# Layer 0 of a two-layer decoder step: the conv-gate and conv-input products of each width tile as seven block products instead of two full ones

## The chip, the core and the metric

The kernel runs on one core of a Trainium2 chip. Its engines have queues of their own: TensorE (PE, matmuls; PEld is its weight load), VectorE (DVE), ScalarE (ACT), GpSimd (POOL) and SyncE (SP, which issues most transfers). The metric is the device time of one execution in microseconds (us), the median of several runs.

## What is computed

One inference step of a trunk of two layers: 512 prompt positions and 8 sample sequences of 8 positions, 576 columns in all, through layer 0 (a gated short convolution) and layer 1 (an mLSTM block). The change is in the input half of layer 0:

```
hnorm = rmsnorm(x, norm_w[0])                             # x: 576 positions x 1024
b_gate, c_gate, xa, z = jnp.split(hnorm @ w_in, 4, -1)    # w_in: 1024 x 8192, 2048 each
u = c_gate * xa
conv, new_buf = causal_dwconv(u, buf, conv_w)             # 3 taps along the positions
y = b_gate * conv * jax.nn.silu(z)
x = x + y @ w_out                                         # w_out: 2048 x 1024
```

All data are fp32.

## The kernel before

Activations lie with 128 features on the partitions and the 576 positions along the free side; 1024 features are 8 such tiles, the width of 2048 is 16 (`NW`). Weights come in chunks of 512 KB (`io["wts"][c]`): 1024 input features by 128 output features. Layer 0 has chunks 0 to 63: width tile f uses chunk 4f for `c_gate`, 4f+1 for `xa`, 4f+2 for `z` and 4f+3 for `b_gate`. Chunks 64 to 79 are its output projection, from 80 on layer 1.

fp32 products are made of three reduced ones (fp32r): each operand is split into a rounded high part and the rest, and hi*hi, hi*lo and lo*hi are added. ScalarE makes the high part of half a chunk (L195, `wh<-wr`, 128x512), VectorE the rest (L196, `wl<-wr,wh`); four such pairs of buffers rotate. A chunk's product (`gemm`, `products`, `step`) is 8 feature tiles by 3 parts by two matmuls of 256 and 320 columns (L210): 48 matmuls into one accumulator `acc` of two PSUM banks. Two accumulators rotate, and loads run ahead in four raw buffers `wr`.

The norm's scale per position is not applied to the input, but as `rb` to products (`rb2`, its square, to `c_gate*xa`). Chunks 0 to 3 are multiplied while the norm is still being summed, and copied to `raws`. Then the loop over f issues, in this order: chunk 4f+4 (`c_rows(f + 1)`, scaled from PSUM to `cr`, L486), chunk 4f+1 (`u = acc * cr`, L504), the convolution of u (L405 to L411), chunk 4f+2 (`z`, L510, silu L511), chunk 4f+3 (`cv = acc * cv`, L513, then times z, L514), and `split(cv)` (L152, L153), which keeps the rows for the output projection.

Layer 1 already uses block products for its v, k and q projections. `gemm_pair` takes two chunks as a 2x2 block matrix (two chunks by even and odd feature tiles) and the activations as another (even and odd feature tiles by first and last 288 positions), for half of the input features; the other half goes the plain way (L340). `forms` prepares sums and differences of the activation blocks, `block_weights` loads the two chunks and makes two sums `ws` (L267, L268), `parts_of` splits a block of weights (L238, L239), and `block_pair` issues the seven products, each 4 tiles by 3 parts by one matmul of 288 columns (L284), and combines the four result blocks with VectorE additions and ScalarE copies of 288 columns.

The order on each engine is set when the program is built: instructions are recorded in the order of the code and placed by a scheduler that has its own idea of their lengths, and each engine then works its queue strictly in that order. PSUM has eight banks: four one-bank buffers in a pool that lasts the whole program (`psum`, tag `b1`), and four banks in a pool that `accumulators` closes and opens again for a stage.

## Time and profile before

| what | before |
|---|---|
| median of 3 runs (range) | 1739.17 us (1736.37 to 1743.02) |
| profiled execution: time / span | 1740.33 us / 1738.2 us |
| granted TensorE clock, mean | 0.987 |
| PE busy / DVE busy / ACT busy | 1694.7 us (97%) / 1005.3 us (58%) / 647.7 us (37%) |
| DMA moved | 275.23 MB, mean 158 GB/s |

The profiled execution is one run, of which every instruction was recorded; it is 1.2 us above the median. A matmul's record is longer than its share of the engine, since matmuls overlap; the price of one is read from starts that follow each other. Layer 0's input half covers about the first 420 us, its output projection the next 100 us (its last rows are stored at 523 us).

### The profile page before, as it was taken

The numbers are of one execution on the slowest core, as the hardware profiler recorded it, in microseconds if no ns is written. First come the engines' busy times: TensorE is split into PE (matmuls) and PEld (weight loads), VectorE is DVE, ScalarE is ACT, GpSimd is POOL, SyncE is SP. The second block draws the span as 40 slices with busy tenths as digits, with TensorE's granted clock in tenths as the row PEclk, the third lists the DMA queues.
The fourth block names the chain that finished last, engine by engine and source line by source line (L and its number), as shares of the span: only waits on it lengthen the run. The fifth ranks groups of instructions, "written<-read, shape, count | busy, mean of one in ns | idle before, by whom it ended". The sixth has DMA issues, their size and how long they took to land. (4 is left out here: it accounts for less than half of the span.)

```text
span 1738.2 us, 30944 instructions
## 1 busy us (share of the span) xinstructions
PE 1694.7 (97%) x12483; PEld 1615.4 (93%) x12483; DVE 1005.3 (58%) x1864; ACT 647.7 (37%) x1172; POOL 104.7 (6%) x241
## 2 busy tenths in 40 slices
PE   9999999999999999999999999999999998998998
PEld 9999999999999999999899989899898787888898
DVE  5644445444335997555755436355367566677755
ACT  5222222222323554333434224233245455555421
POOL 0000000000001000000111010100011000000000
PEclk9999999999999999999999999999999899999999
DMA  5232222222432435344432463452745588797973
GB/s 190 86 93 76 87 89 86 92 76 95 140 126 93 129 107 176 107 150 122 152 116 95 150 203 118 168 175 85 240 159 203 170 289 288 251 327 268 366 287 104
DMA packets 107487, 275.23 MB, mean 158 GB/s; under 512 B 11057, under 2 KB 33457, under 8 KB 107345
## 3 DMA queue, kind: packets, MB, share of 16 engines
q1 hardware_dynamic: 91984, 255.95, 44.7%
q10 hardware_dynamic: 15360, 17.32, 2.9%
q8 instruction: 98, 1.61, 0.4%
q14 instruction: 45, 0.36, 0.1%
HBM read 211.13 MB, written 62.09 MB: 157 GB/s over the span
## 5 line engine op out<-in xcount | busy, mean ns | idle before, releaser
L210 PE MATMUL acc<-hi,wh 128*128 128x256 f32 (+1 forms) x1968 | 427.8, 299 | 10.0 <-ACT z L804 6.8
L210 PE MATMUL acc<-hi,wl 128*128 128x256 f32 (+1 forms) x1968 | 426.3, 298 | 0.0
L210 PE MATMUL acc<-lo,wh 128*128 128x256 f32 (+1 forms) x1968 | 425.7, 298 | 0.0
L195 ACT CAST wh<-wr 128x512 fp32r<-128x512 f32 x342 | 211.1, 620 | 514.4 <-PE acc L210 396.9
L210 PEld LDWEIGHTS acc<-hi,wh 128*128 128x128 f32 x1968 | 333.5, 191 | 14.5 <-ACT z L804 7.0
L196 DVE TENSOR_TENSOR wl<-wr,wh 128x512 fp32r<-128x512 f32 x342 | 234.1, 688 | 188.2 <-ACT wh L195 183.2
L210 PEld LDWEIGHTS acc<-hi,wl 128*128 128x128 f32 x1968 | 332.8, 191 | 2.8 <-issue 1.7
L210 PEld LDWEIGHTS acc<-lo,wh 128*128 128x128 f32 x1968 | 333.2, 191 | 0.7 <-issue 0.5
L284 PE MATMUL p<-hi,wh 128*128 128x288 f32 x576 | 171.1, 301 | 0.9 <-DVE xm L557 0.9
L340 PE MATMUL p<-hi,wh 128*128 128x288 f32 x736 | 170.2, 299 | 0.0
L284 PE MATMUL p<-lo,wh 128*128 128x288 f32 x576 | 169.2, 295 | 0.0
L284 PE MATMUL p<-hi,wl 128*128 128x288 f32 x576 | 166.1, 295 | 1.2 <-DVE wl L239 1.2
L340 PE MATMUL p<-lo,wh 128*128 128x288 f32 x736 | 167.3, 295 | 0.0
L340 PE MATMUL p<-hi,wl 128*128 128x288 f32 x736 | 166.7, 297 | 0.2 <-DVE wl L196 0.2
L340 PEld LDWEIGHTS p<-hi,wh 128*128 128x128 f32 x736 | 121.1, 188 | 14.7 <-issue 11.2
L340 PEld LDWEIGHTS p<-hi,wl 128*128 128x128 f32 x736 | 121.1, 188 | 4.6 <-issue 2.9
L238 ACT CAST wh<-wr 128x512 fp32r<-128x512 f32 x96 | 59.6, 620 | 175.1 <-PE p L340 117.4
L340 PEld LDWEIGHTS p<-lo,wh 128*128 128x128 f32 x736 | 121.8, 188 | 0.0
L284 PEld LDWEIGHTS p<-hi,wh 128*128 128x128 f32 x576 | 108.0, 188 | 5.0 <-ACT k L329 2.5
L284 PEld LDWEIGHTS p<-lo,wh 128*128 128x128 f32 x576 | 108.5, 188 | 0.0
L284 PEld LDWEIGHTS p<-hi,wl 128*128 128x128 f32 x576 | 107.1, 188 | 1.4 <-DVE wl L239 1.4
L1052 DVE SCALAR_TENSOR_TENSOR c<-c,cols,r 128x512 f32<-128x512 f32 x128 | 91.1, 743 | 27.2 <-PE r L1051 21.0
(363 smaller groups left out, 2276.3 us busy)
## 6 DMA issues: line engine op xcount, KB each, us to landing
wr<-wts SPq DMA_DIRECT2D x222, 512.0 KB, 3.6
c<-cs SPq DMA_DIRECT2D x112, 512.0 KB, 5.8
cs_out<-c SPq DMA_DIRECT2D x64, 512.0 KB, 6.6
x<-xT SPq DMA_DIRECT2D x16, 288.0 KB, 4.2
xcs<-xc ACTq DMA_DIRECT2D x16, 288.0 KB, 2.1
x<-xcs SPq DMA_DIRECT2D x16, 288.0 KB, 4.1
x<-x1s SPq DMA_DIRECT2D x16, 288.0 KB, 4.8
ld<-xcs SPq DMA_DIRECT2D x16, 288.0 KB, 8.4
```

The source lines that it names most:

```text
L195: last_act[0] = nc.scalar.copy(hi, raw[:, 4 * i:4 * i + 4, :]).ins
L196: nc.vector.tensor_tensor(lo, raw[:, 4 * i:4 * i + 4, :], hi.bitcast(F32), ALU.subtract)
L210: nc.tensor.matmul(acc[:, o:o + j - i], a[:, k % 4, :], x[:, i:j], start=(first and k == 0 and p == 0), stop=(last and k == 7 and p == 2))
L238: last_act[0] = nc.scalar.copy(hi, src).ins
L284: nc.tensor.matmul(bank_, a[:, j, :], x, start=(start and j == 0 and i == 0), stop=(j == 3 and i == 2), skip_group_check=True)
L340: nc.tensor.matmul(b, a[:, k % 4, :], x[:, t:t + HT], start=bool(new) and k == 0 and i == 0, stop=(k == 7 and i == 2), skip_group_check=True)
L1052: ins = nc.vector.scalar_tensor_tensor(ct[:, j, :], ct[:, j, :], dec[:, o + j:o + j + 1], r, ALU.mult, ALU.add).ins
```

## The change

Width tile 0 stays as it was. Chunks 4 and 5 are made as before, but copied to scratch tiles `cx`. For the width tiles 2 to 15, chunks 4f and 4f+1 are made by one `block_pair` over all 1024 input features (`xs=None`: no plain part), one f ahead, and its four result blocks fill the two tiles `cx`. Since both factors now lie in SBUF, `gated` scales and multiplies them there; it and the steps of the convolution are put in a list `work`, from which `block_pair` takes one after each of five of its products. Chunks 4f+2 and 4f+3 stay plain products of 48 matmuls.

The activation blocks that the seven products need are made at the start of the layer (`first_blocks`, four times, from x times the norm's weight). The program-wide PSUM pool is gone: the one-bank buffers belong to each stage's pool, and layer 0 has three pools in turn, `acc0` up to chunk 5, `acc0a` (two accumulators and four one-bank blocks) for the loop, and `acc0b` from the output projection on. Scratch tiles of layer 0 (`X`, seven buffers) lie in the pool of the load buffers, which is closed and opened again at the output projection.

```diff
-        psum = ctx.enter_context(tc.tile_pool(name="psum", bufs=4, space=PSUM))
+        layer0 = [False]
+        def X(n=NT, name="x"):
+            if not layer0[0]:
+                return T(n, name=name)
+            uid[0] += 1
+            return loads[1].tile([P, n], F32, name=f"{name}{uid[0]}", tag="X", bufs=7)
...
-            return psum.tile([P, 512], F32, name=f"{name}{uid[0]}", tag="b1", bufs=4)
+            return accs[1].tile([P, 512], F32, name=f"{name}{uid[0]}", tag="b1", bufs=4)
...
+        def mixed(xa, xb):
             a, b = T(name="fa"), T(name="fb")
             nc.vector.tensor_tensor(a[:, 0:HT], xa[:, 0:HT], xa[:, HT:NT], ALU.subtract)
             nc.vector.tensor_tensor(a[:, HT:NT], xb[:, HT:NT], a[:, 0:HT], ALU.add)
             nc.vector.tensor_tensor(b[:, 0:HT], xa[:, HT:NT], xb[:, HT:NT], ALU.subtract)
             nc.vector.tensor_tensor(b[:, HT:NT], xb[:, 0:HT], a[:, HT:NT], ALU.subtract)
+            return split(a), split(b)
...
-        def block_pair(c1, c2, fs, xs, out1, out2, add, mid=None, then=None):
+        def block_pair(c1, c2, fs, xs, out1, out2, add, mid=None, then=None, pops=0):
...
             product(b0, parts_of(a11), "b11", True)
             nc.scalar.copy(p, b0)
+            run(pops)
...
+            elif xs is None:
+                nc.scalar.copy(o11, b0)
+                tt(o21, b3, u, ALU.add)
...
+        def first_blocks(j):
+            for x, i in ((xs[2 * j], 2 * j), (xs[2 * j + 1], 2 * j + 1)):
+                nc.vector.tensor_scalar(x, x, col("norm0", i), None, ALU.mult)
+            b11 = [x[:, 0:HT] for x in h1[2 * j]]
+            fs.append(blocks_of(*mixed(xs[2 * j], xs[2 * j + 1]), b11, h1[2 * j + 1]))
...
         raw_product(mm("acc"), w2)
         rc = [rms_columns([ssq[:, 288 * i:288 * i + 288]], 96) for i in range(2)]
+        first_blocks(0)
         raw_product(mm("acc"), w3)
...
+        first_blocks(1)
...
         for f in range(NW):
...
+            work.append(gated)
+            work.extend(conv_steps(cv, u, ext_f, [col("ca0", f), col("ca1", f), col("ca2", f)]))
+            work.append(saved)
+            zb = [raw_weights(4 * f + i) for i in (2, 3)] if f else None
+            if f + 1 < NW:
+                cx = [X(name="cx") for _ in range(2)]
+            if f == 0:
+                for i in range(2):
+                    acc = mm("acc")
+                    products(acc, weights(4 + i), h1, True, True)
+                    nc.scalar.copy(cx[i], flat(acc))
+                    if i:
+                        block_weights(8, 9)
+                    first_blocks(2 + i)
+                accumulators("acc0a", bufs=2)
+            elif f + 1 < NW:
+                block_pair(4 * f + 4, 4 * f + 5, fs, None, *cx, False, pops=1)
+            run(len(work))
+            if 0 < f < NW - 2:
+                block_weights(4 * f + 8, 4 * f + 9)
...
-            cr = next_cr
-            if f + 1 < NW:
-                next_cr = c_rows(f + 1)
-            xa = product(1)
...
+        accumulators("acc0b", bufs=2)
+        load_buffers("loads1", 4)
+        layer0[0] = False
```

The built program shows what stands where. On PE the rows go from 11857 to 11689. The first place is VectorE's queue in the middle of the loop, from the row that reads the `b_gate` product out of PSUM. In a row, `wl<-wr,wh` is the low half of a plain or block weight, `lo` that of the finished rows. Before:

```order
L513 TENSOR_TENSOR cv_1973<-acc_2044,cv_1973 128x576
L196 TENSOR_TENSOR wl_2178<-wr_2171,wh_2177 128x512
L514 TENSOR_TENSOR cv_1973<-cv_1973,z_2040 128x576
L153 TENSOR_TENSOR lo_2106<-cv_1973,hi_2105 128x576
L196 TENSOR_TENSOR wl_2243<-wr_2240,wh_2242 128x512
L486 TENSOR_TENSOR cr_2109<-acc_2110,rb_470 128x576
L196 TENSOR_TENSOR wl_2247<-wr_2240,wh_2246 128x512
L196 TENSOR_TENSOR wl_2306<-wr_2303,wh_2305 128x512
L504 TENSOR_TENSOR u_2229<-acc_2170,cr_1851 128x576
L196 TENSOR_TENSOR wl_2310<-wr_2303,wh_2309 128x512
L406 COPY ext_1333<-u_2229 128x8x8
L409 SCALAR_TENSOR_TENSOR cv_2231<-u_2229,cols,cv_2231 128x511
```

And now at the same place (`ws` are the weight sums, `pu` and `p` the scratch and a PSUM block of `block_pair`):

```order
L581 TENSOR_TENSOR cv_2075<-acc_2287,cv_2075 128x576
L251 TENSOR_TENSOR wl_2417<-wr_2219,wh_2416 128x512
L582 TENSOR_TENSOR cv_2075<-cv_2075,z_2284 128x576
L251 TENSOR_TENSOR wl_2438<-wr_2220,wh_2437 128x512
L160 TENSOR_TENSOR lo_2347<-cv_2075,hi_2346 128x576
L542 TENSOR_TENSOR u_2350<-cx_2081,cx_2080 128x576
L251 TENSOR_TENSOR wl_2457<-wr_2220,wh_2456 128x512
L319 TENSOR_TENSOR cx_2356<-pu_2358,p_2359 128x288
L437 COPY ext_1520<-u_2350 128x8x8
L326 TENSOR_TENSOR cx_2357<-pu_2358,p_2396 128x288
L251 TENSOR_TENSOR wl_2477<-ws_2224,wh_2476 128x512
L440 SCALAR_TENSOR_TENSOR cv_2351<-u_2350,cols,cv_2351 128x511
```

The four plain splits of this stretch are now four splits of block weights, the scaled `cr` has gone, and two result blocks `cx` have come between u and the convolution.

The second place is VectorE's queue at the start of the layer, from the row of the squared scale `rb2`. Before, a plain split and the first gated rows followed it:

```order
L479 TENSOR_TENSOR rb_470<-rb_451 128x576
L196 TENSOR_TENSOR wl_627<-wr_620,wh_626 128x512
L486 TENSOR_TENSOR cr_473<-raw_307,rb_470 128x576
L486 TENSOR_TENSOR cr_477<-acc_478,rb_470 128x576
L504 TENSOR_TENSOR u_538<-raw_309,cr_473 128x576
```

Now two rows follow it, `rb_499<-rb_464` at L527 itself and the first of the mixed activation blocks (`fa_570<-x_127`, L257), and then these, up to the second weight sum `ws` of the first pair of chunks:

```order
L259 TENSOR_TENSOR fb_571<-x_127,x_129 128x288
L541 TENSOR_TENSOR raw_304<-raw_304,rb_499 128x576
L541 TENSOR_TENSOR cx_506<-cx_506,rb_499 128x576
L258 TENSOR_TENSOR fa_570<-x_129,fa_570 128x288
L260 TENSOR_TENSOR fb_571<-x_129,fa_570 128x288
L160 TENSOR_TENSOR lo_577<-fa_570,hi_576 128x576
L160 TENSOR_TENSOR lo_581<-fb_571,hi_580 128x576
L257 TENSOR_TENSOR fa_654<-x_131 128x288
L259 TENSOR_TENSOR fb_655<-x_131,x_133 128x288
L286 TENSOR_TENSOR ws_648<-wr_645 128x512
L258 TENSOR_TENSOR fa_654<-x_133,fa_654 128x288
L287 TENSOR_TENSOR ws_649<-ws_648,wr_644 128x512
```

The two last pairs of mixed blocks `fa` and `fb`, their low halves `lo` and the two sums `ws` have moved in front of the first weights of the first block product.

More of the change, by code (lines that the diff above doesn't have):

```diff
@@ L197, in split_weights, with raw_weights, weights @@
             return hi, lo
-        def weights(chunk, keep=False):
+        def raw_weights(chunk):
             raw = weight_tile()
             latest[0] = load(out=raw, in_=io["wts"][chunk]).ins
+            return raw
+        def weights(chunk, keep=False, raw=None):
+            if raw is None:
+                raw = raw_weights(chunk)
             return [split_weights(raw, i, keep) for i in range(2)]
@@ L298, in block_pair @@
                 tt(o12, p, b1, ALU.subtract)
+            run(pops)
             product(b0, parts_of(a12), "b21", False)
@@ L399, in rms_spread, with conv_steps, first, tap @@
             return acc
-        def conv(cv, u, ext, taps):
+        def conv_steps(cv, u, ext, taps):
             n = len(taps)
             h = n - 1
-            nc.scalar.activation(cv, u, AF.Copy, scale=taps[h])
-            nc.vector.tensor_copy(ext[:, :, h:h + 8], u[:, NP:NT].rearrange("p (b t) -> p b t", t=8))
             cs = cv[:, NP:NT].rearrange("p (b t) -> p b t", t=8)
-            for s in range(1, n):
+            def first():
+                nc.scalar.activation(cv, u, AF.Copy, scale=taps[h])
+                nc.vector.tensor_copy(ext[:, :, h:h + 8], u[:, NP:NT].rearrange("p (b t) -> p b t", t=8))
+            def tap(s):
                 nc.vector.scalar_tensor_tensor(cv[:, s:NP], u[:, 0:NP - s], taps[h - s], cv[:, s:NP],
@@ L411, in conv @@
                 nc.vector.scalar_tensor_tensor(cs, ext[:, :, h - s:h - s + 8], taps[h - s], cs, ALU.mult, ALU.add)
+            return [first] + [lambda s=s: tap(s) for s in range(1, n)]
+        def conv(*args):
+            for go in conv_steps(*args):
+                go()
         load(out=cols, in_=io["cols"])
```

48 lines of the change are left out of this document (28 added, 20 removed).

## The prediction

> **What bounds the kernel now.** I read the page first, then the busy times by stretch, then the stage of the change in time order. Columns of the stretches: length, busy us (and instructions) of PE, PEld, DVE, ACT, POOL, granted clock, DMA share, GB/s.
>
> ```profile
> PE 1694.7 (97%) x12483; PEld 1615.4 (93%) x12483; DVE 1005.3 (58%) x1864; ACT 647.7 (37%) x1172; POOL 104.7 (6%) x241
> 100.00:200.00 100.00, 100.00 (x752) 100.00 (x752) 48.32 (x80) 28.35 (x44) 2.32 (x4) 1.00 0.28 87
> 200.00:300.00 100.00, 100.00 (x752) 100.00 (x752) 47.17 (x79) 27.09 (x42) 2.32 (x4) 1.00 0.28 84
> 640.00:660.00 20.00, 18.65 (x135) 17.79 (x134) 20.00 (x47) 10.64 (x18) 0.00 (x0) 1.00 0.33 113
> 820.00:840.00 20.00, 20.00 (x155) 20.00 (x154) 14.82 (x30) 8.95 (x17) 0.00 (x0) 1.00 0.49 165
> 860.00:880.00 20.00, 20.00 (x154) 20.00 (x153) 17.61 (x35) 8.85 (x16) 4.03 (x8) 1.00 0.43 126
> ```
>
> In the stage of the change (100 to 300 us) PE never stops at full clock, VectorE is busy under half the time, DMA a quarter. So a matmul taken away is time taken away, as long as its replacement keeps PE fed. The last three rows lie in layer 1, where the same block products run: PE stays full with VectorE 74% and 88% busy, and loses 1.35 of 20 us only with VectorE busy all the time. That is the scale for what follows.
>
> **PE's share of the change.** A pair of plain products is 2 x 48 matmuls of 288 columns on average; seven block products are 7 x 12 = 84 of 288. Fourteen width tiles change: 14 x 12 = 168 matmuls go, the difference of PE's rows in the built program (11857 to 11689). A plain one costs 100 / 752 = 0.133 us. A block one, from the starts in layer 1:
>
> ```profile
> 657.40 0.29 PE L284 MATMUL p<-lo,wh 128*128 128x288 f32 x1
> ...
> 658.47 0.29 PE L284 MATMUL p<-hl,wl 128*128 128x288 f32 x1
> ```
>
> Eight steps in 1.07 us, 0.134 each: the same. The gain is 168 x 0.133 = **22.3 us**, 1.6 per pair, if PE stays full.
>
> **VectorE in the loop.** Records overlap, so I price it from starts that follow each other without idle:
>
> ```profile
> 631.13 0.75 DVE L153 TENSOR_TENSOR lo<-xm,hi 128x576 fp32r<-128x576 f32 x1
> 631.80 0.75 DVE L409 SCALAR_TENSOR_TENSOR xc<-xm,cols,xc 128x511 f32<-128x511 f32 x1
> 632.46 0.28 DVE L411 SCALAR_TENSOR_TENSOR xc<-ext,cols,xc 128x64 f32<-128x64 f32 x1
> 632.65 0.69 DVE L239 TENSOR_TENSOR wl<-wr,wh 128x512 fp32r<-128x512 f32 x1
> ...
> 637.50 0.69 DVE L196 TENSOR_TENSOR wl<-wr,wh 128x512 fp32r<-128x512 f32 x1
> 638.10 0.69 DVE L268 TENSOR_TENSOR ws<-ws,wr 128x512 f32<-128x512 f32 x1
> ...
> 641.02 0.46 DVE L310 TENSOR_TENSOR pu<-p,pu 128x288 f32<-128x288 f32 x1
> 641.39 0.45 DVE L314 TENSOR_TENSOR v<-p,v 128x288 f32<-128x288 f32 x1
> ```
>
> So 0.67 us for 576 columns, 0.60 for 512, 0.37 for 288, 0.66 and 0.20 for the convolution's two kinds. Per width tile before: 8 weight splits, 7 rows of 576, 4 convolution rows and a copy (0.1): 4.8 + 4.7 + 1.8 = 11.3 us of 192 x 0.133 = 25.5. After: 11 splits (7 block, 4 plain) and 4 weight sums, 15 x 0.60 = 9.0; six block additions 2.2; seven rows of 576 4.7; convolution 1.8: 17.7 us of 180 x 0.133 = 23.9, 74%. ScalarE gets 3 more casts and two copies of 288: at most 3 x 0.62 + 2 x 0.40 = 2.7 us per tile on an engine busy 28%, no bound. DMA moves the same bytes.
>
> A share of 74% still needs slack at each place. Put t = 0 where PE begins a pair. It runs p6, p1, p5 (1.6 each, split during the plain products), the first two matmuls of p4 (to 5.1), the second halves of p1 (to 6.6), p4 (8.0), p6 (9.6), p5 (11.2), then z (17.6) and b_gate (23.9). VectorE at t = 0 stands at the read of the b_gate accumulator (L581, the first row shown in the order): it can't pass it before PE is done, and four block splits are queued behind it. Adding up from 0.2: L581 to 0.9, split of a12 to 1.5, L582 2.1, a21 2.7, the finished rows 3.4 (behind a cast), u 4.1, a22 4.7, two result blocks and a copy, s2 6.1. PE wants them at 5.1, 8.0, 6.6 (a22's low half) and 9.6: the tightest, a22, has 1.9 us, about 1.4 if the cast makes VectorE wait. The two plain splits (7.6 and 9.6) are wanted at 11.2 and 14.4. So nothing waits; I take 0.5 us for the whole loop, between 0 and the upper end of the second rival.
>
> The loads: a raw buffer is free when a22 is split (t = 4.7); SP then issues the next pair's second chunk, which L286 (the first weight sum) reads at 8.4.
>
> ```profile
> DMA to landing us min/median/max: 3.3/3.5/4.4
> ```
>
> It lands at 8.0 to 9.1 (the weight loads from 40 to 400 us). VectorE may wait 0.7 there, with a plain split behind it that has 4.8 us of slack: hidden. If a landing took over 8 us, PE would wait. SP's order otherwise only shifts; the loads of chunks 65 to 67 stand behind `cpa_out`, which waits for POOL's copy from u(15), made 12 us before. POOL's work is the same.
>
> **The seam at the start.** Sixteen block rows, eight scalings and eight splits of the mixed blocks (16 x 0.37 + 16 x 0.67 = 16.6 us, a scaling priced like the other rows of 576) are new on VectorE ahead of the first pair, where it was busy 15.5 of 28 us:
>
> ```profile
> 21.00:49.00 28.00, 28.00 (x218) 28.00 (x218) 15.53 (x31) 11.14 (x21) 1.86 (x3) 1.00 0.26 83
> 41.88 0.39 PE L210 MATMUL acc<-lo,wh 128*128 128x320 f32 x1
> 42.57 0.76 DVE L479 TENSOR_TENSOR rb<-rb 128x576 f32<-128x576 f32 x1 [2.71 <-ACT rb L477]
> ```
>
> PE's order up to chunk 5 is unchanged; after the second norm spread (41.88) 51 matmuls remain, so PE is free at 48.7. VectorE starts `rb2` at 42.57, and 14 rows stand from it to the second weight sum: five of 576, seven of 288, two of 512 = 7.1 us, ready at 49.8 with its pipeline. A cast (0.62) later, 50.4, p6 can start: PE waits 1.7. Then three products get two matmuls each until p6's low half is split (four more rows, 2.2 us, at 52.0): another 0.8. Together 2.5, and I take **2.7 us** with wake-ups; the ends are 0 (if VectorE gets to `rb2` with nothing left over and the sums are made sooner) and 8 (if it keeps the pace of the row above, 15.5 of 28, on these rows: 7.1 / 0.55 = 12.9). I stay near the sum of the rows, since only two of the 14 wait for another engine.
>
> The Trainium skill ("VectorE: DVE Perf Modes", section "The DRAIN you can't avoid") says that after each VectorE op the next doesn't start until the pipeline is empty, unless it is not held. By whole records (0.69 for 512) the chain of 14 would be some 1.2 us longer and the sum 1.2 us worse; the rows above, 0.60 apart with 0.69 recorded, speak against it here.
>
> **The seam at the output projection.** Chunk 64's accumulator now belongs to a new pool, and its first matmul waits for VectorE's read of chunk 63's accumulator; before, two accumulators rotated and that read was hidden.
>
> ```profile
> 420.18 0.76 DVE L513 TENSOR_TENSOR cv<-acc,cv 128x576 f32<-128x576 f32 x1 [2.08 <-PE acc L210]
> PE ta L609 <- ACT ta L613: 2.2, 1, 2.2
> ```
>
> At least its 0.76; the largest wait of PE behind an evacuation in layer 1 is 2.2. I take **1.1**, near the row itself plus two hand-overs. The load of chunk 64 waits for the old load pool, whose last reader is u(15), 12 us earlier: hidden. The seam `acc0` to `acc0a` waits for chunk 5's last matmul, which is in front of it on PE anyway. Later stages keep their work.
>
> Sum: -22.3 + 0.5 + 2.7 + 1.1 = -18.0 us. The profiled execution took 1740.3 (span 1738.2 and 2.1 around it), 1.2 above the median of 1739.17; against that median, **1721 us**, likely 1716 to 1726.
>
> **Rivals.** *The start seam trips the clock.* In layer 1 PE once ran dry for 2.2 us (the last row above), did a few transposes and waited 1.4 more:
>
> ```profile
> PE tb L611 <- DVE tb L614: 1.4, 1, 1.4
> PE p L284 <- DVE wl L239: 1.2, 1, 1.2
> 850.00:852.00 2.00, 0.34 (x2) 0.34 (x3) 2.00 (x4) 2.00 (x4) 0.00 (x0) 0.96 0.00 0
> 852.00:854.00 2.00, 0.64 (x4) 0.25 (x3) 1.97 (x5) 1.12 (x3) 0.00 (x0) 0.50 0.59 166
> 854.00:856.00 2.00, 1.98 (x12) 1.67 (x16) 1.23 (x3) 2.00 (x5) 0.00 (x0) 0.50 0.69 196
> 856.00:858.00 2.00, 2.00 (x17) 0.51 (x17) 1.98 (x5) 1.43 (x5) 0.00 (x0) 0.50 0.82 229
> ```
>
> The clock stood at 0.50 for some 6 us, of which PE worked 4.6: 2.3 us lost. My seam is a wait of 1.7 us and a sparse 1.6: near it, but the wait of 1.2 us, between 640 and 660, cost no clock (1.00 in the row at the top). It would give 1723. Chance 0.2. The Trainium skill ("TensorE: Matmul & The Clock Gate", section "What's actually happening") has the clock halved after an idle window of about 3.4 us whose phase is free; by that rule it could go either way, and the 0.50 agrees.
>
> *VectorE becomes the bound, slower than before.* All block splits stand behind L581 in one queue. If VectorE ran late by over 1.9 us at a22 in each pair, every pair would stall. Priced by 640 to 660 us (PE 18.65 of 20): 23.9 / 0.9325 = 25.7, 1.7 per pair, 24 us: 1721 + 24 = 1745. It ends above the old time from 1.3 us per pair ((22.3 - 3.8) / 14). Against it: 74% of the period, and the rows at 74% and 88% with PE full. Chance 0.07.
>
> *Half of that:* late loads or casts cost some 0.7 us per pair, 10 us: 1731. For it speaks the 0.7 us by which a load can be late for L286. Chance 0.13.
>
> *The seams are hidden:* ends 0 and 0.76, loop 0: 1718 or lower. Chance 0.1. That the change takes no matmuls away is excluded by the rows of the program.
>
> **Numbers.** My forecast 0.5, the clock 0.2, the half stall 0.13, VectorE 0.07, hidden seams 0.1. Half a per cent, about what a measurement of this kernel can tell, is 8.7 us: faster means under 1730.5. The forecast, the clock and the hidden seams all are (0.8), and of the half stall a third (0.04): 0.84. The rest of it (0.09) and half of VectorE's case (0.03) end within, 0.12; its other half is slower, 0.04. The range 1715 to 1730 holds the forecast, the clock and the hidden seams and leaves out about 2 in 10.
>
> **What would show it.** Right: from 100 to 400 us PE full at about 752 matmuls per 100 us, VectorE some 80% busy; a pair of products 11.2 us long and a width tile 23.9; a PE wait of 2 to 3 us near 50 us that ends at a cast `wh<-ws`, one of about 1 us near 400 us that ends at L581; the first rows of the output projection stored 18 us sooner and all later stages moved by the same. Wrong: waits of PE for `wl` or `wh` in each width tile; L286 waiting for loads of over 5 us; a clock under 1.00 after the first seam; or a later stage, slower for its new PSUM pools, that gives the gain back.

## The result and the profile after

The changed kernel takes **1715.8 us** in the median of five runs (1713.1 to 1717.8), the kernel before 1737.9 beside it: ratio 0.9872 (95% interval 0.9857 to 0.9887). Forecast were 18.0 us less, by the medians it is 22.1 (by the interval of the ratio 19.6 to 24.9), and 1715.8 lies at the lower edge of the range 1715 to 1730. The profiled execution took 1715.6 us, its span 1713.5.

The same views as before the change, the page's first line:

```profile
PE 1669.4 (97%) x12315; PEld 1591.1 (93%) x12315; DVE 1105.3 (65%) x2078; ACT 685.3 (40%) x1252; POOL 107.7 (6%) x241
```

and the busy times by stretch (length; PE, PEld, DVE, ACT, POOL; granted clock, DMA share, GB/s):

```profile
100.00:200.00 100.00, 100.00 (x755) 100.00 (x755) 76.29 (x137) 39.64 (x68) 2.34 (x4) 1.00 0.30 90
200.00:300.00 100.00, 100.00 (x756) 100.00 (x755) 77.62 (x142) 40.65 (x70) 2.93 (x5) 1.00 0.31 95
```

168 matmuls have gone (12483 to 12315), PE is full at full clock as before, and VectorE went from 48% to 77% of the time. How long a width tile lasts is read from a row that comes once in each, the product `u`; VectorE's timeline, before and after:

```profile
106.58 0.76 DVE L504 TENSOR_TENSOR u<-acc,cr 128x576 f32<-128x576 f32 x1 [2.08 <-PE acc L210]
132.18 0.76 DVE L504 TENSOR_TENSOR u<-acc,cr 128x576 f32<-128x576 f32 x1 [2.08 <-PE acc L210]
```

```profile
104.52 0.75 DVE L542 TENSOR_TENSOR u<-cx,cx 128x576 f32<-128x576 f32 x1
128.43 0.75 DVE L542 TENSOR_TENSOR u<-cx,cx 128x576 f32<-128x576 f32 x1
```

25.60 us became 23.91: 1.69 per tile, 23.7 for the fourteen.

Where along the program did the time go? Three transfers mark places of it: the first rows of the output projection (`x1s`), the store of the convolution's rows in layer 1 (`cpb_out`) and the first stored state rows (`kps`). The numbers before the last semicolon are the starts of the first and last of such transfers. Before, then after:

```profile
L528 SPq DMA_DIRECT2D x1s<-x x8: 327/327/327, 433.8 to 523.4; - x8
L573 SPq DMA_DIRECT2D cpb_out<-cpb x1: 344/344/344, 630.3 to 630.3; - x1
L615 ACTq DMA_DIRECT2D kps<-ta x16: 326/326/327, 875.6 to 1313.2; - x16
```

```profile
L599 SPq DMA_DIRECT2D x1s<-x x8: 327/327/327, 415.6 to 505.2; - x8
L644 SPq DMA_DIRECT2D cpb_out<-cpb x1: 344/344/344, 612.5 to 612.5; - x1
L686 ACTq DMA_DIRECT2D kps<-ta x16: 326/326/327, 854.4 to 1290.2; - x16
```

Layer 0 gave 18.2 us (433.8 to 415.6), still 17.8 at `cpb_out`. But at `kps` it is 21.2: a stretch of layer 1 that the change was not said to touch takes 241.9 us instead of 245.3.

Such places also move with the start of the kernel. PE's first matmul behind the second norm spread stood at 41.88 before (the row is in the prediction) and now stands later:

```profile
42.13 0.39 PE L222 MATMUL acc<-lo,wh 128*128 128x320 f32 x1
```

In the fourteen profiles of this case it stands between 41.19 and 42.50. Counted from it, the first store comes 391.88 us later in each of the four kernels with the old layer 0, and 373.47 us later in the changed one: layer 0 gave 18.4 us. "Counted from the spread" below means this count.

The start seam, in the timelines of PE, ACT and DVE:

```profile
48.76 0.43 PE L222 MATMUL acc<-hi,wl 128*128 128x256 f32 x2
51.26 0.40 PE L304 MATMUL p<-hi,wh 128*128 128x288 f32 x1 [2.07 <-ACT wh L250]
55.05 0.42 PE L304 MATMUL p<-hi,wl 128*128 128x288 f32 x2
...
49.22 0.64 ACT L559 COPY cx<-acc 128x576 f32<-128x576 f32 x1 [1.91 <-PE acc L222]
50.59 0.62 ACT L250 CAST wh<-ws 128x512 fp32r<-128x512 f32 x1
...
42.82 0.76 DVE L527 TENSOR_TENSOR rb<-rb 128x576 f32<-128x576 f32 x1 [1.60 <-ACT rb L524]
49.81 0.68 DVE L287 TENSOR_TENSOR ws<-ws,wr 128x512 f32<-128x512 f32 x1
```

and by stretches:

```profile
49.00:52.00 3.00, 0.93 (x5) 0.52 (x4) 3.00 (x6) 2.71 (x5) 0.00 (x0) 0.92 0.00 0
52.00:55.00 3.00, 3.00 (x13) 2.98 (x14) 3.00 (x6) 1.34 (x3) 0.00 (x0) 0.51 0.02 5
```

PE waits 2.07 us for the cast of the second weight sum, and then the clock is at half until 55: 13 matmuls in 3 us, where 22 fit. The other seam is one row of PE's waits (total, times, longest), at chunk 64:

```profile
PE acc L222 <- DVE cv L581: 0.9, 1, 0.9
```

Between the two PE has no wait.

### The profile page after: what moved, and what is told of

Read it like the earlier page. It is cut to its first block, busy times and chain, and to the rows that moved or that the text cites. A ratio compares the mean times of both kernels' runs of the same rounds, so it can differ in the third digit from the quotient of the medians.

```text
span 1713.5 us, 30944 instructions
## 1 busy us (share of the span) xinstructions
PE 1669.4 (97%) x12315; PEld 1591.1 (93%) x12315; DVE 1105.3 (65%) x2078; ACT 685.3 (40%) x1252; POOL 107.7 (6%) x241
## 4 chain that ended last, share of the span: by engine, by line
PE 88%; DMA 5%; DVE 4%; ACT 2%; issue 1%; SPq 0%; POOL 0%; DVEq 0%; ACTq 0%; POOLq 0%
PE acc L222 34%; PE p L304 24%; PE p L368 16%; DMA c<-cs 2%; PE qa L759 2%; PE r L1122 2%; DMA cs_out<-c 1%; DMA wr<-wts 1%; PE g L661 1%; PE num L1175 1%; PE ta L680 1%; PE cp L1175 1%; PE num L1176 1%; PE s L778 1%; PE blk L368 1%
## 5 line engine op out<-in xcount | busy, mean ns | idle before, releaser
L222 PE MATMUL acc<-hi,wh 128*128 128x256 f32 (+1 forms) x1520 | 331.7, 299 | 11.1 <-ACT z L875 6.8
L222 PE MATMUL acc<-hi,wl 128*128 128x256 f32 (+1 forms) x1520 | 330.8, 299 | 0.0
L222 PE MATMUL acc<-lo,wh 128*128 128x256 f32 (+1 forms) x1520 | 330.2, 299 | 0.0
L304 PE MATMUL p<-hi,wh 128*128 128x288 f32 x968 | 286.7, 299 | 3.7 <-ACT wh L250 2.1
L304 PE MATMUL p<-lo,wh 128*128 128x288 f32 x968 | 284.5, 295 | 0.0
L304 PE MATMUL p<-hi,wl 128*128 128x288 f32 x968 | 279.2, 295 | 1.2 <-DVE wl L251 1.2
L222 PEld LDWEIGHTS acc<-hi,wh 128*128 128x128 f32 x1520 | 257.8, 191 | 16.0 <-ACT z L875 7.0
L222 PEld LDWEIGHTS acc<-hi,wl 128*128 128x128 f32 x1520 | 257.8, 191 | 2.2 <-issue 1.2
L222 PEld LDWEIGHTS acc<-lo,wh 128*128 128x128 f32 x1520 | 257.7, 191 | 0.7 <-issue 0.5
L368 PE MATMUL p<-hi,wh 128*128 128x288 f32 x736 | 169.9, 299 | 0.0
L368 PE MATMUL p<-lo,wh 128*128 128x288 f32 x736 | 166.9, 294 | 0.0
L368 PE MATMUL p<-hi,wl 128*128 128x288 f32 x736 | 166.4, 296 | 0.2 <-DVE wl L203 0.2
L251 DVE TENSOR_TENSOR wl<-ws,wh 128x512 fp32r<-128x512 f32 x114 | 78.7, 691 | 119.6 <-ACT wh L250 119.4
```

The source lines that it names most:

```text
L222: nc.tensor.matmul(acc[:, o:o + j - i], a[:, k % 4, :], x[:, i:j], start=(first and k == 0 and p == 0), stop=(last and k == 7 and p == 2))
L251: nc.vector.tensor_tensor(lo, src, hi.bitcast(F32), ALU.subtract)
L304: nc.tensor.matmul(bank_, a[:, j, :], x, start=(start and j == 0 and i == 0), stop=(j == 3 and i == 2), skip_group_check=True)
L368: nc.tensor.matmul(b, a[:, k % 4, :], x[:, t:t + HT], start=bool(new) and k == 0 and i == 0, stop=(k == 7 and i == 2), skip_group_check=True)
```

## The experiments

Two questions were open: whether layer 0 gave its 18.2 us for the reasons of the sum, and where the rest came from. In each diff `-` is the kernel it starts from. Medians of the kernel before differ by up to 3.3 us between the sets of runs, so small edits are read from the profile; there a place in layer 0 can stand about a microsecond off from one profile to the next, unless it is counted from the spread.

**Half of the pairs.** From the changed kernel:

```
-            elif f + 1 < NW:
+            elif f + 1 < NW and f % 2 == 0:
+                for i in range(2):
+                    acc = mm("acc")
+                    products(acc, weights(4 * f + 4 + i), h1, True, True)
+                    nc.scalar.copy(cx[i], flat(acc))
+            elif f + 1 < NW:
                 block_pair(4 * f + 4, 4 * f + 5, fs, None, *cx, False, pops=1)
             run(len(work))
-            if 0 < f < NW - 2:
+            if 0 < f < NW - 2 and f % 2 == 0:
                 block_weights(4 * f + 8, 4 * f + 9)
```

> The changed kernel with the block products in every second width tile only: seven pairs instead of fourteen, the other seven as plain products whose accumulators ScalarE copies out. Pools, loads and rows stay. Theory (the gain is the matmuls taken away, 12 per pair at 0.133 us, 1.6 us per pair): PE has 84 matmuls more than the changed kernel, the first store of the output projection moves from 415.6 to 426.8, the time rises by 11.2 us, and no wait of PE appears in the loop. Rival (part of the loop's gain comes from the order of the work, the pools or the interleaving): the store moves by less than 9 us; or the plain tiles bring waits of their own, and it moves by more than 13.

VectorE's timeline:

```profile
106.80 0.75 DVE L542 TENSOR_TENSOR u<-cx,cx 128x576 f32<-128x576 f32 x1
130.71 0.76 DVE L542 TENSOR_TENSOR u<-cx,cx 128x576 f32<-128x576 f32 x1
156.31 0.75 DVE L542 TENSOR_TENSOR u<-cx,cx 128x576 f32<-128x576 f32 x1
```

In this kernel a tile of 23.91 us stands next to one of 25.60, with pools, loads and rows alike. So a pair is worth 1.69 us, a little more than 12 x 0.133, and the gain in the loop comes from the matmuls, not from the pools or the order. The first store comes at 428.0, 12.4 us later than with all pairs, 12.2 counted from the spread (7 x 1.69 = 11.8); the time is 1726.0, ratio 0.9909 (0.9876 to 0.9942).

**Room on VectorE: rows on unused data.** From the changed kernel, with a `junk` tile that nothing reads:

```
+        def more(go):
+            def both():
+                go()
+                for _ in range(2):                     # 4 in the second kernel
+                    nc.vector.tensor_tensor(junk, junk, rb[:, :288], ALU.mult)
+            return both
...
+            if f:
+                for i in range(len(work)):
+                    work[i] = more(work[i])
```

> The changed kernel with ten added VectorE rows of 288 columns on unused data in each width tile from the second on, two behind each of the five steps that are put between the block products: 10 x 0.37 = 3.7 us, which takes VectorE from 17.7 to 21.4 of a tile's 23.9 us (89%; up to 100 to 300 us at 92 busy, by records). Theory (the slack at each place is what I added up: tightest the low half of a22 with 1.9 us; the two rows ahead of a22 that belong to a step are 0.74 to 1.5 us): no wait or waits of less than 0.3 us per tile, the first store moves by under 3 us. Rival (VectorE is nearly the bound): each pair loses over 0.5 us, the first store comes at 423 or later.

> The changed kernel with twenty added VectorE rows of 288 columns on unused data in each width tile from the second on, four behind each of the five steps between the block products: 20 x 0.37 = 7.4 us, VectorE 25.1 us for a tile of 23.9. Theory (by the rows' prices VectorE is then the bound): a tile lasts 25.1 us or more, fourteen tiles cost 14 x 1.2 = 17 us or more, and the first store moves from 415.6 to 432 or later (to 445 if each pair also stalls at a22 and the clock falls), so that nearly all of the gain is lost: this prices the room that the change had. Rival (the prices are too high, rows of 288 on full records overlap more than I have it): under 8 us lost.

The stretches of the loop, the kernel with ten rows first, then two of the kernel with twenty:

```profile
100.00:200.00 100.00, 100.00 (x755) 100.00 (x754) 91.28 (x182) 39.59 (x68) 5.31 (x5) 1.00 0.29 88
```

```profile
100.00:200.00 100.00, 100.00 (x755) 100.00 (x754) 91.34 (x181) 39.27 (x68) 4.95 (x4) 1.00 0.29 88
400.00:420.00 20.00, 18.94 (x143) 18.73 (x142) 18.06 (x37) 6.38 (x10) 0.00 (x0) 1.00 0.50 170
```

With ten rows VectorE is busy 91% and PE loses nothing in the loop; the first store comes at 417.6 (the time is 1718.1), the 2.0 us being a start seam of 3.1 us instead of 2.1, since nine of the unused rows were put ahead of it, and a longer half clock behind it. The kernel with twenty tells nothing more of the loop: it has as many VectorE rows between 100 and 200 us as the one with ten (181 and 182). The order of the program had put the unused rows behind the loop, where VectorE is still busy at 400 to 420 us. The expected 432 or later did not come (416.8; the time is 1719.2), because the edit did not load the loop as intended.

**Room on VectorE: rows in the chain.** So the twenty rows were tied to the tile's own data:

```
+                for i in (0, 288, 0, 288):
+                    nc.vector.tensor_tensor(t[:, i:i + 288], t[:, i:i + 288], ones, ALU.mult)
...
+                    work[i] = more(work[i], cv if i else u)
```

> The changed kernel with twenty more VectorE rows of 288 columns in each width tile from the second on, four behind each of the five steps between the block products; each multiplies the half of u or cv that the step made by one, so the rows lie in the chain of the tile's own work and can't be put off behind the loop, as rows on unused data were. VectorE gets 20 x 0.37 = 7.4 us more, 25.1 us for a tile whose matmuls take 23.9. Theory (rows at the prices of the sum; VectorE is the bound from about 6 us more per tile): VectorE is busy 98% or more from 100 to 400 us, PE falls below 755 matmuls in 100 us to 720 or fewer, PE waits in each tile, and the first store of the output projection comes at 432 us or later. Rival (rows overlap more than priced, and the room is larger): the store comes before 424 us.

A stretch of the loop, and the two largest of PE's waits in layer 0:

```profile
100.00:200.00 100.00, 95.57 (x704) 93.61 (x703) 97.56 (x204) 35.94 (x62) 2.52 (x4) 1.00 0.28 88
```

```profile
PE acc L222 <- DVE cv L594: 25.1, 14, 11.3
PE acc L222 <- DVE z L592: 6.1, 8, 0.8
```

Now VectorE is the bound: PE does 704 matmuls in 100 us instead of 755 and waits for VectorE's reads of the accumulators. The first store comes at 460.1, and the time is 1764.1, ratio 1.0141 (1.0122 to 1.0161): slower than the kernel with no block products in layer 0. More than I expected, since a backlog of 11.3 us was left for the output projection to wait for. So the change had room for 3.7 us of VectorE work per tile, and with 7.4, in this place, it turns into a loss. These rows also lengthen the chain of each tile, which the unused ones did not; with VectorE busy 98% the load alone leaves no room.

**The clock at the start seam.** From the changed kernel:

```
+                with tc.issue_after(last_mm[0]):       # the last matmul of chunk 5
+                    seam = warm_up(18)
...
+                with tc.issue_after(seam) if f == 1 else nullcontext():
                     block_pair(4 * f + 4, 4 * f + 5, fs, None, *cx, False, pops=1)
```

> The changed kernel with 18 matmuls on unused data between chunk 5's last matmul and the first block product, so that PE works through its wait of 2.1 us near 49 us. Nothing else is changed. Theory (the wait halved the clock for about 3 us, which cost 1.3 us): the clock is 1.00 from 49 to 58 us, 13 matmuls in 52 to 55 us become over 20, the first store of the output projection moves from 415.6 to 414.3, the time by -1.3 us. Rival (the clock fell for another reason, or the matmuls that were slow would have waited for weights anyway): 0.50 stays, or the first store stays at 415.6 within 0.3 us although the clock is full.

The stretch in question, and the first store:

```profile
52.00:55.00 3.00, 3.00 (x21) 2.71 (x21) 3.00 (x6) 1.76 (x4) 0.00 (x0) 1.00 0.00 0
```

```profile
L604 SPq DMA_DIRECT2D x1s<-x x8: 326/326/326, 414.4 to 504.0; - x8
```

The clock stays at 1.00 and the first store comes 1.2 us sooner (1.3 expected), 0.9 counted from the spread. With the wait filled the half clock is gone, so it came of the wait, though a wait of this length doesn't always bring it (see the kernel with the accumulators kept). The median, 1715.2 (ratio 0.9862, 0.9842 to 0.9882), is too coarse to show it.

**The order at the start seam.** From the changed kernel:

```
-        nc.vector.tensor_tensor(rb2, rb, rb, ALU.mult)
...
+                r45 = [raw_weights(4 + i) for i in range(2)]
                 for i in range(2):
                     acc = mm("acc")
-                    products(acc, weights(4 + i), h1, True, True)
+                    products(acc, weights(4 + i, raw=r45[i]), h1, True, True)
                     nc.scalar.copy(cx[i], flat(acc))
-                    if i:
+                    if not i:
                         block_weights(8, 9)
                     first_blocks(2 + i)
+                with tc.issue_after(last_lo[0]):
+                    nc.vector.tensor_tensor(rb2, rb, rb, ALU.mult)
```

> The changed kernel with the order at the start seam altered: the weight sums of the first block pair are made before the last two additions of mixed blocks instead of behind the first of them, and rb2 is made behind those additions instead of ahead of all 14 rows. The same instructions, other order. Theory (the seam is VectorE's queue of 14 rows ahead of the second weight sum): PE's wait at the first block product falls from 2.1 us to under 0.5, the clock stays at 1.00, the sparse stretch stays or grows by at most 1 us, and the first store of the output projection comes 2 to 3.4 us sooner, near 413; the time is 2 to 3.4 us less than the changed kernel's. Rival (the seam is the loads or the casts of ScalarE): the wait stays above 1.5 us.

PE's timeline at the first block product, and the first store:

```profile
49.59 0.40 PE L305 MATMUL p<-hi,wh 128*128 128x288 f32 x1 [1.04 <-ACT cx L560]
```

```profile
L602 SPq DMA_DIRECT2D x1s<-x x8: 327/327/327, 412.2 to 501.8; - x8
```

3.4 us sooner, of which 0.6 lie ahead of the seam: counted from the spread (41.50 here) it is 2.7, within what was expected. Of that 1.0 is wait and 1.7 the half clock and the sparse stretch. So most of the seam was VectorE's queue. The wait isn't gone, though (under 0.5 was expected). It is 1.04 us and ends elsewhere: at ScalarE's copy of chunk 5's accumulator to `cx`. The clock stays at 1.00. The median, 1715.1, moved less than the first store did.

**The loop's accumulators kept through the output projection.** From the changed kernel, without the pool `acc0b` (the scratch banks take the tag `blk`):

```
-            return accs[1].tile([P, 512], F32, name=f"{name}{uid[0]}", tag="b1", bufs=4)
+            return accs[1].tile([P, 512], F32, name=f"{name}{uid[0]}", tag="blk" if in_a[0] else "b1", bufs=4)
...
-        accumulators("acc0b", bufs=2)
```

> The changed kernel without the new accumulator pool at the output projection: chunk 64 on goes on in the pool of the loop, whose accumulator rotates with the others. Theory (the first matmul of chunk 64 waits 0.9 us for VectorE's read of the accumulator of chunk 63, only because the pool is new): that wait is gone and the first store comes 0.9 us sooner, at 414.7. Rival: the read is waited for in any case, since the finished rows that the projection multiplies are made from it and PE runs out of other work; then a wait of 0.5 us or more stays within some us of that place and the store stays at 415.6.

The stretch behind the start seam, and the first store:

```profile
52.00:55.00 3.00, 3.00 (x23) 2.93 (x23) 3.00 (x6) 1.35 (x4) 0.00 (x0) 1.00 0.03 8
```

```profile
L600 SPq DMA_DIRECT2D x1s<-x x8: 326/326/326, 412.8 to 502.4; - x8
```

The wait of 0.9 us is gone, and the first store comes 2.8 us sooner, not 0.9. Of this 0.7 lie ahead of the start seam (the spread is at 41.40, the first block product starts at 50.53), 1.1 are the seam of the output projection by PE's starts, and 1.0 is the clock, which was not halved here although PE waited 2.1 us at the start all the same. The kernel as a whole is no faster than the changed one (1721.3, 1720.9 to 1728.8; ratio 0.9905, 0.9883 to 0.9927): its later waits are other ones, of which the largest are 8.1 us of PE for `kst` (2.4 in the changed kernel). Why the later stages came out so stays open.

**Both edits:**

> The changed kernel with both seams taken away: the weight sums of the first pair ahead of the last additions of mixed blocks and rb2 behind them, and the loop's accumulators kept through the output projection. Theory: both gains of the single edits add, the first store comes 3 to 4.3 us sooner than the changed kernel's 415.6, at 411.3 to 412.6, and the time falls by the same, to about 1712. Rival (a seam that PE doesn't meet at one place it meets at the next): less than 2 us sooner.

The first store:

```profile
L603 SPq DMA_DIRECT2D x1s<-x x8: 326/326/326, 411.0 to 500.6; - x8
```

4.6 us sooner than 415.6 and **1711.1 us**, ratio 0.9835 (0.981 to 0.986): the lowest median here. Counted from the spread it is 3.9 us sooner, the 2.7 of the order and the 1.1 of the pool; both seams can be had.

**Banks by stage alone.** From the kernel before:

```
-        psum = ctx.enter_context(tc.tile_pool(name="psum", bufs=4, space=PSUM))
...
-            return psum.tile([P, 512], F32, name=f"{name}{uid[0]}", tag="b1", bufs=4)
+            return accs[1].tile([P, 512], F32, name=f"{name}{uid[0]}", tag="b1", bufs=4)
```

> The kernel before with one edit: the four rotating result banks come from the pool of each stage instead of one pool for the whole program. No product is changed. The first rows of the output projection are stored at 433.8 us before and at 415.6 after; from there to the first stored state rows of layer 1 (875.6 and 854.4) another 3.0 us goes, which my sum did not hold. Theory: these 3.0 us come from the banks by stage, which let the transposes of layer 1 near 850 us start without the wait of 2.2 us on ScalarE and the halved clock behind it; then the first store stays at 433.8 within 1 us (seams of the new pools cost up to 1), PE's waits at the transposes fall from 3.6 us to about 2.5, the clock there stays at 1.00, and the whole is 2 to 4 us faster, ratio about 0.998. Rival: the 3.0 us come from where the stages fall in time after layer 0 got shorter; then the stall at the transposes is 3.6 us with the clock at 0.50 as before, and the time is 0 to 2 us slower, ratio 1.000 to 1.001.

PE's waits at the last transposes of layer 1's v:

```profile
PE ta L608 <- ACT ta L612: 2.0, 1, 2.0
PE tb L610 <- DVE tb L613: 1.5, 1, 1.5
```

1738.5 against 1738.8, ratio 1.0 (0.9984 to 1.0016). The stall at the transposes stays with its half clock (0.50), the stretch from `cpb_out` to `kps` is 245.0 us. The banks are not where the extra gain came from.

**The order of hl in layer 1.** The change reaches into layer 1 after all: `forms`, which layer 1 calls, was taken apart into `mixed` and `blocks_of`, and the first block (`hl`) is now written behind the splits of the two mixed blocks. On ScalarE and VectorE of layer 1 this order is the only difference of weight. It was put into the kernel before, and taken out of the changed one:

```
             nc.vector.tensor_tensor(b[:, HT:NT], xb[:, 0:HT], a[:, HT:NT], ALU.subtract)
+            (ah, al), (bh, bl) = split(a), split(b)
             o = R(name="hl")
             nc.scalar.copy(o[:, 0:HT], xa[:, 0:HT])
             nc.vector.tensor_tensor(o[:, HT:NT], xa[:, 0:HT], o[:, 0:HT].bitcast(F32), ALU.subtract)
-            (ah, al), (bh, bl), (xh, xl) = split(a), split(b), split(xb)
+            xh, xl = split(xb)
```

and in the changed kernel, where `first_half` holds the two hl rows:

```
-        def mixed(xa, xb):
+        def mixed(xa, xb, between=None):
...
+            if between:
+                between()
             return split(a), split(b)
...
-            a, b = mixed(xa, xb)
+            a, b = mixed(xa, xb, first_half)
```

> The kernel before with one edit in forms: the copy and the remainder of the first block (hl) are written behind the splits of the two mixed blocks instead of ahead of them, as the change writes it too. Layer 0 is as before. Theory (4.6 to 4.9 us that layer 1 took less in six kernels with the change, and 3.4 in the changed kernel's profile, come from this order alone): from the store of the convolution's rows (630.3 us before) to the first stored state rows of layer 1 it takes 240.4 to 242 us instead of 245.3, PE's waits of 2.2 and 1.4 us at the transposes ta and tb fall to under 1 us each, the clock there stays at 1.00, the first store of the output projection stays at 433.8, and the time falls by 3 to 5 us, ratio about 0.998. Rival (the stage took less for another reason, its pools or its place in time): 245 us as before, clock 0.50 near 852 us, ratio 1.000.

> The changed kernel with that one edit undone: hl again ahead of the splits of the two mixed blocks; layer 0 as changed. Theory: the first store of the output projection stays at 415.6 us within 0.3, the stretch from the store of the convolution's rows to the first state rows goes back to 245 us with the halved clock in it, and the time rises by 3 to 5 us to about 1720, 18 us under the kernel before: what the sum of layer 0 alone gave. Rival: the stretch stays at 240 to 242 us and the time at 1716.

The kernel before with the new order, first state rows and PE's waits at the last transposes:

```profile
L616 ACTq DMA_DIRECT2D kps<-ta x16: 326/326/348, 873.4 to 1310.2; - x16
```

```profile
PE tb L612 <- DVE tb L615: 1.5, 1, 1.5
PE ta L610 <- ACT ta L614: 0.8, 1, 0.8
```

With `cpb_out` at 630.4 the stretch is 243.0 us, 2.3 less instead of 3.3 to 4.9, and the clock there still falls to 0.50. Its time did not move (1741.2 against 1740.2, ratio 1.0003, 0.999 to 1.0015). The changed kernel with the old order:

```profile
L691 ACTq DMA_DIRECT2D kps<-ta x16: 326/326/326, 853.4 to 1290.7; - x16
```

```profile
PE tb L687 <- DVE tb L690: 1.7, 1, 1.7
```

From `cpb_out` at 612.2 it is 241.2 us, not 245: the theory fails there. The time is 1720.0, ratio 0.9883 (0.9867 to 0.9899), which the interval of the changed kernel overlaps. So the order of hl is a part of it at most.

**The loads in front of the stall.** In the kernel before, VectorE's first row on the last two x, and SP's queue ahead of it, from the timelines:

```profile
847.86 0.46 DVE L245 TENSOR_TENSOR fa<-x 128x288 f32<-128x288 f32 x1 [3.75 <-DMA x<-xcs]
...
836.98 5.97 SPq L264 DMA_DIRECT2D wr<-wts  x2
843.04 1.74 SPq L164 DMA_DIRECT2D x<-xcs  x2
```

VectorE waits 3.75 us for x, whose load stands behind two weight loads, the second of which had to wait for a buffer. That can be taken away. From the kernel before:

```
-            for j in range(4):
-                fc.append(forms(later_tile(2 * j), later_tile(2 * j + 1)))
+            pairs = [[later_tile(2 * j), later_tile(2 * j + 1)] for j in range(2)]
+            for j in range(4):
+                if j + 2 < 4:
+                    pairs.append([later_tile(2 * j + 4), later_tile(2 * j + 5)])
+                fc.append(forms(*pairs[j]))
```

> The kernel before with one edit in layer 1: the loads of x for the mixed blocks in the last pair of v are issued two pairs of tiles ahead, so that the last four stand before the last weight loads on SP's queue and not behind them. Layer 0 is as before. Theory (the stall at the transposes ta and tb hangs on the last two x, which are issued 212.7 us behind the store of the convolution's rows, because the weight load in front of them waits for a buffer, and land at 217.6): they land before 212, PE's waits at ta and tb fall from 3.6 us to under 1.5, the clock stays at 1.00, and the stretch to the first state rows falls from 245.3 us to 240 to 241.5, what the kernels with the changed layer 0 show; the time falls by 3 to 5 us. Rival (the casts and splits of the mixed blocks on VectorE and ScalarE are late whatever the loads do, or the weights behind the loads now come late): 243 us or more.

SP's timeline, and the first state rows:

```profile
817.53 2.75 SPq L164 DMA_DIRECT2D x<-xcs  x6
826.87 0.86 SPq L164 DMA_DIRECT2D x<-xcs  x2
834.04 0.33 SPq L264 DMA_DIRECT2D wr<-wts  x1
```

```profile
L615 ACTq DMA_DIRECT2D kps<-ta x16: 326/326/327, 869.7 to 1305.6; - x16
```

The x loads now come before the weights, PE has no wait at ta and tb, the clock stays at 1.00, and the stretch (`cpb_out` at 630.9) is 238.8 us, 6.5 less. The time follows: 1730.8 against 1737.4, ratio 0.9965 (0.995 to 0.998). The stall hangs on these loads. In the changed kernel with the old order of hl the same row starts sooner, counted from `cpb_out`: 827.39 - 612.2 = 215.2 us instead of 847.86 - 630.3 = 217.6, and that was enough to keep the clock up:

```profile
827.39 0.46 DVE L257 TENSOR_TENSOR fa<-x 128x288 f32<-128x288 f32 x1 [2.95 <-DMA x<-xcs]
```

That the loads come sooner goes with the changed layer 0 in all ten kernels that have it (240.4 to 241.9 us; 245.0 and 245.3 with the old layer 0 and the old order). It isn't the order of the queues: SP's is the same in the kernel with hl back as before, VectorE's and ScalarE's are but for a few neighbouring rows, and PE's matmuls stand within 0.25 us of the same places up to the stall. What differs is how long loads take to land. The pair of x loads ahead of the last one, before and with hl back:

```profile
DMA to landing us min/median/max: 7.2/7.3/7.4
DMA to landing us min/median/max: 4.7/4.9/5.0
```

VectorE's row on them waits 2.26 us before and 0.26 with hl back, so, counted from `cpb_out`, the weight split behind it comes 1.5 us later. That split frees the buffer that the weight load at 836.98 waits for, and so this load and the last x behind it come 1.5 us later too. In the kernel with banks by stage it is the last pair itself that takes longer (with hl back 4.0 to 4.3):

```profile
DMA to landing us min/median/max: 6.5/6.7/6.8
```

Why the same loads take longer there stays open. In the table, the row on x is the first of VectorE on the last two x, counted from `cpb_out`:

| kernel | layer 0 | hl | row on x, us | `cpb_out` to `kps`, us | PE's waits at the last ta and tb, us | lowest clock there |
|---|---|---|---|---|---|---|
| before | old | first | 217.5 | 245.3 | 3.6 | 0.50 |
| banks by stage | old | first | 217.3 | 245.0 | 3.5 | 0.50 |
| hl behind | old | behind | 215.9 | 243.0 | 2.3 | 0.50 |
| changed | new | behind | 215.4 | 241.9 | 0.6 | 1.00 |
| hl back | new | first | 215.2 | 241.2 | 1.7 | 1.00 |
| x loads early | old | first | 210.2 | 238.8 | 0 | 1.00 |

The stretch follows the row on x, whatever layer 0 and the order of hl are. The other eight kernels with the change fit in: 212.8 to 214.2 us, and a stretch of 240.4 to 240.5.

## Why the prediction was right, and where it was off

**The end of layer 0 came out as summed, by errors that cancel.** Forecast -18.0, measured 433.8 - 415.6 = 18.2, or 18.4 counted from the spread. That the sum met it so closely is in part luck. Its terms:

- *The matmuls taken away, -22.3.* Measured 14 x (25.60 - 23.91) = -23.7. The number of matmuls was right, the price low: 192 plain ones take 25.60, 0.1333 each; of 23.91 the 96 plain ones take 12.80 and the 84 block ones 11.11, 0.1323 each. I priced all by 0.133 and so missed that the block ones are 1% shorter.
- *The loop, +0.5.* Measured 0: no wait of PE between the seams. The slack held as added up, and ten more rows of 288 per tile still fitted. I could have taken 0.
- *The start seam, +2.7.* Measured about 3.9, of two kinds. The wait is 2.07 us (1.7 forecast): the 14 rows of VectorE took 7.67 us instead of 7.2, of which 0.25 are a wait for ScalarE's cast of `fa`, and the cast of the second sum began 0.1 us late, behind another cast on ScalarE. (`rb2` started 0.25 us later than the row of before, but so did PE's matmuls behind the spread.) And the rival *the start seam trips the clock* came true: from 51.26 to 55.05 PE started 15 matmuls, which take 2.0 us at full clock, so 1.8 were lost, with the sparse stretch. I had given it 0.2 and 2.3 us. Keeping the clock up brought 0.9.
- *The out-projection seam, +1.1.* Measured 0.94, with the row I had named; taking the pool away takes the wait away. The bound beside it was misread: 2.2 us is not PE's largest wait behind an evacuation in layer 1. PE's waits before also show one for a row of ScalarE that reads an accumulator into `z`:

```profile
PE acc L210 <- ACT z L804: 6.8, 1, 6.8
```

The 1.1 did not rest on it.

That is -23.7 + 3.9 + 0.9 = -18.9. These waits run from the end of a record to the next start. From start to start, less the 0.13 of one matmul, the two seams cost 2.25 (48.88 to 51.26) and 1.12 (400.49 to 401.74), and the sum is -23.7 + 2.25 + 1.8 + 1.1 = -18.5 against the 18.4 counted from the spread; the other 0.25 us are the later start. One thing said of the seams was wrong: that `acc0` to `acc0a` waits only for chunk 5's last matmul. It waits for ScalarE's copy of that accumulator as well, which was hidden behind VectorE's queue and showed as 1.04 us when that queue was made shorter.

**The step that failed is "later stages keep their work".** The work is kept, but not the stall of 3.6 us near 850 us with 2.3 us of half clock behind it, which I had quoted in a rival and counted as fixed. In the changed kernel 0.6 of that wait is left, and the clock stays up. It hung on loads behind a weight load that waits for a buffer; the diff's new order in `forms`, and loads that land sooner in the kernels with the shorter layer 0, each bring them a little forward. In the profiles this is 3.4 us. What lies behind the first `kps` can't be told from one profile: from there to the end the fourteen take 855 to 869 us (862.6 before, 859.1 changed), and twelve runs of the kernel with banks by stage went from 1733.6 to 1745.2. So the 22.1 by the medians is 18 from layer 0, some 3 from this stall, and a rest that is within the noise.

**The rivals that did not come.** VectorE did not become the bound (77% busy, as the row at 74% had suggested), and no load was late in the loop. The rows in the chain show that the rival was real: with 7.4 us more per tile the change is a loss.

**Records or starts, and the length of the wait.** The Trainium skill, "VectorE: DVE Perf Modes", section "The DRAIN you can't avoid", read without its exception for ops that are not held, would have let each of the 14 rows at the seam last to the end of its record. From 42.82 to 50.49 they took 7.67 us with one gap of 0.25; the records of the 14 sum to 8.3. The trace keeps siding with the starts. The Trainium skill, "TensorE: Matmul & The Clock Gate", section "What's actually happening", has the clock halved after an idle window of about 3.4 us, free-running. Here it fell after an idle time of 2.07 us, less than such a window, and not after 2.08 us of waiting in the kernel with the accumulators kept: the free phase agrees with the trace, the length as a threshold does not. The half clock lasted some 3.5 us (51.5 to 55.05), about the length of one window.

## What to carry to other kernels

Where PE is full, a product traded for fewer matmuls is worth its matmuls, and the profile tells beforehand whether the engine that pays for it has room; count that room by place and not by share alone. Here the seams cost more than the loop: list for the first row of a new phase everything that must come off each queue ahead of it, copies out of the old accumulators included. Two profiles of nearly the same program can stand a microsecond apart from the start on, so count places from a row that no edit touches. And a helper that is taken apart for one stage is also called by another: a stall that hangs on a late load can shrink or grow by several microseconds from such a shift, so stalls of the profile before should carry a range of their own, and an edit that removes one is worth trying by itself (here 6.5 us for five lines).

## What was not expected of the hardware

A wait of PE of 2.1 us at the start seam halved the granted clock in four kernels and not in a fifth with the same wait: from 52 to 55 us it was 0.51 in the changed kernel, 0.60 with half of the pairs, 0.55 with hl back and 0.60 with the rows in the chain, and 1.00 with the accumulators kept. Two loads of the same size, at the same place of the program, took 4.9 us to land in one kernel and 7.3 in another, and a stall of layer 1 moved with it. And VectorE rows on data that nothing reads did not stay where they were written: the order of the program moved half of them out of the loop, as the counts by stretch show. That is the scheduler's doing, not the chip's.
